# Issuing each half store of the first fourteen sequences as two DMAs of 64 partitions

## Chip, cores, metric

One core of a Trainium2 chip. The metric is the device time of one execution in microseconds, the slowest core's; here there is only one. The "span" of a profile is the part of it that the profiler records, from the first recorded instruction to the last.

## The reference

```python
# indices (32, 512) int32, embedding_table (50000, 512) f32, position_embed (512, 512) f32
def reference(indices, embedding_table, position_embed):
    token_embed = embedding_table[indices]
    return (token_embed + position_embed).astype(np.float32)
```

33.6 MB are gathered in rows of 2 KB, one addition is made on each element, and 33.6 MB are written. The tables and the result lie in HBM ("dram" in the names of the trace); the slots that the gathers fill and the stores read are tiles in SBUF, laid out over 128 partitions (an addition in the trace is 128x512).

## The kernel before

Position p * 4 + k of a sequence lies on partition p. GpSimd issues 128 gathers of 128 rows, VectorE adds the position embedding in place, and the queue of the scalar engine (ScalarE, "ACT") issues the stores. Most stores are "half stores": two of the four k of one sequence, 4 KB on each of 128 partitions, 512 KB.

```python
P = 128; K = 4; SLOTS = 23; LANES = 10; FIRST = 4
# ... tiles, loads of indices and position embedding ...
stores = []
for g, (b, k) in enumerate(order):
    if (b <= 1 and k < half) or b == B - 1:
        stores.append((g + 1, b, k, 1))
    elif k % half == half - 1:
        stores.append((g + 1, b, k + 1 - half, half))
# ...
for g, (b, k) in enumerate(order):                 # GpSimd
    # ... waits for indices; at b == SLOTS for the stores of the slots that are reused
    ins = nc.gpsimd.indirect_dma_start(out=slots[b % SLOTS][:, k, :], in_=table, ...)
    if g >= LANES:
        ins._wait_ge(s_gather[g % LANES], rounds(g - LANES))
# ...
for g, (b, k) in enumerate(order):                 # VectorE
    part = slots[b % SLOTS][:, k, :]
    nc.vector.tensor_tensor(out=part, in0=part, in1=pos_ps[:, k, :], op=add) # waits for gather g
# ...
for adds, b, at, n in stores:                      # ScalarE's queue
    nc.scalar.dma_start(
        out=out_rows[b][:, at : at + n, :],
        in_=slots[b % SLOTS][:, at : at + n, :],
    )._wait_ge(s_add, adds).then_inc(done, 16)
```

## Time and profile before

| | before |
|---|---|
| time, median (3 runs) | 182.06 us |
| span of the profile | 178.8 us |
| GpSimd / VectorE busy | 68% / 51% |
| DMA engines busy, steady stretch | 100% |
| data moved | 68.34 MB, about 418 GB/s from 40 us on |

The prediction below shows the lines behind this table. One more line is needed, the stores as instructions of ScalarE's queue. It reads: line, engine, operation, tile, count, duration of an issue in ns (shortest/median/longest), first and last start in us.

```profile
L160 ACTq DMA_DIRECT2D out_dram<-slot x68: 338/338/372, 8.8 to 170.9; - x68
```

The issues take 338 ns, the longest 372.

### The profile page before, as it was taken

The page shows a single profiled execution, that of the slowest core. Times are in us where ns is not written, and L with a number is a line of the kernel's source. Part 1 is how long each engine was busy: PE and PEld are TensorE (multiplying, and loading weights), DVE is VectorE, ACT ScalarE, POOL GpSimd, SP SyncE. Part 2 cuts the span into 40 slices and gives each one's busy share as a digit, 9 for nine tenths or more (in the row PEclk, how much of TensorE's full clock was granted, in tenths as well). Part 3 has the DMA queues.
Part 4 walks back from the last instruction along what each step waited for, and adds up shares of the span by engine and source line. Part 5 has one row for each costly group of instructions (what it writes and reads, how often), then busy time and mean ns, then how long its engine had stood idle before and what let it go on. Part 6 is the DMA issues. An engine that isn't in the chain of part 4 may idle for free.

```text
span 178.8 us, 399 instructions
## 1 busy us (share of the span) xinstructions
DVE 90.5 (51%) x133; POOL 121.4 (68%) x132
## 2 busy tenths in 40 slices
DVE  0363835555455555555465564556556464555510
POOL 3777777777777777777777777777777777773000
DMA  4999999999999999999999999999999999999950
GB/s 128 305 276 346 331 388 389 411 401 422 415 420 416 419 418 419 420 418 416 420 418 419 418 418 420 414 418 418 420 415 419 420 406 419 417 421 418 414 203 0
DMA packets 21059, 68.34 MB, mean 382 GB/s; under 512 B 3776, under 2 KB 3904, under 8 KB 21056
## 3 DMA queue, kind: packets, MB, share of 16 engines
q0 software_dynamic: 10240, 33.56, 48.3%
q10 hardware_dynamic: 10816, 34.76, 48.3%
q14 instruction: 3, 0.02, 0.0%
HBM read 34.75 MB, written 33.55 MB: 382 GB/s over the span
## 4 chain that ended last, share of the span: by engine, by line
POOL 65%; issue 23%; DMA 6%; DVE 1%; POOLq 1%; ACTq 0%
POOL slot L126 65%; DMA slot<-in_embedding_table_dram,idx_t 5%; DVE slot L151 1%; DMA idx<-in_indices_dram 1%; POOLq L134 1%; ACTq L191 0%; POOLq L97 0%; POOLq L180 0%
## 5 line engine op out<-in xcount | busy, mean ns | idle before, releaser
L126 POOL DMA_INDIRECT slot<-in_embedding_table_dram,idx_t x112 | 105.9, 946 | 34.1 <-issue 34.1
L151 DVE TENSOR_TENSOR slot<-slot,pos_ps 128x512 f32<-128x512 f32 x128 | 87.7, 688 | 75.1 <-issue 61.0
L126 POOL DMA_INDIRECT slot<-in_embedding_table_dram,idx x16 | 15.2, 953 | 7.1 <-issue 4.7
L146 DVE COPY pos_ps<-pos_sb 128x512 f32<-128x512 f32 x4 | 2.8, 688 | 5.2 <-DMA pos_sb<-in_position_embed_dram 5.2
L139 DVE STREAM_TRANSPOSE idx_t<-idx_raw 128x128 int32<-128x128 int32 x1 | 0.4, 401 | 0.0
L180 POOL MEMSET const-float32-0.0<- 128x1 f32 x1 | 0.1, 98 | 0.2 <-issue 0.2
L180 POOL MEMSET const-uint8-127<- 128x1 uint8 x1 | 0.1, 118 | 0.0
L180 POOL MEMSET const-bfloat16-1.0<- 128x1 bf16 x1 | 0.1, 113 | 0.0
L180 POOL MEMSET const-float32-1.0<- 128x1 f32 x1 | 0.1, 104 | 0.0
## 6 DMA issues: line engine op xcount, KB each, us to landing
out_dram<-slot ACTq DMA_DIRECT2D x60, 512.0 KB
out_dram<-slot ACTq DMA_DIRECT2D x8, 256.0 KB
slot<-in_embedding_table_dram,idx_t POOLq DMA_INDIRECT x112
pos_sb<-in_position_embed_dram ACTq DMA_DIRECT2D x2, 512.0 KB
slot<-in_embedding_table_dram,idx POOLq DMA_INDIRECT x16
idx_raw<-in_indices_dram ACTq DMA_DIRECT2D x4, 32.0 KB
idx<-in_indices_dram ACTq DMA_DIRECT2D x1, 4.0 KB, 1.6
idx<-in_indices_dram ACTq DMA_DIRECT2D x1, 12.0 KB
```

The costliest lines, as they stand in the source:

```text
L126: ins = nc.gpsimd.indirect_dma_start(out=slots[b % SLOTS][:, k, :], out_offset=None, in_=table, in_offset=bass.IndirectOffsetOnAxis(ap=whe ...
L134: nc.gpsimd.drain()
L139: nc.vector.transpose(out=idx_t[:], in_=idx_raw[:].rearrange("r (q k w) -> r k q w", k=K, w=2)[:, :, :, 0],)._wait_ge(s_raw, 16 * J).then_ ...
L146: nc.vector.tensor_copy(out=pos_ps[:, k, :], in_=pos_sb[:, k, :])._wait_ge(s_pos[k // half], 16).then_inc(s_ps, 1)
L151: nc.vector.tensor_tensor(out=part, in0=part, in1=pos_ps[:, k, :], op=add)._wait_ge(s_gather[g % LANES], rounds(g)).then_inc(s_add, 1)
L180: nc = _bacc.Bacc("TRN2", target_bir_lowering=False, num_devices=1)
```

## The change

The likely intent is finer pieces of store traffic between the gathers while the pipeline fills. Each half store of sequences 0 to 13 becomes two DMAs, one of partitions 0 to 63 and one of 64 to 127.

```diff
+SPLIT = 14
 ...
-            stores.append((g + 1, b, k, 1))
+            stores.append((g + 1, b, k, 1, slice(0, P)))
         elif k % half == half - 1:
-            stores.append((g + 1, b, k + 1 - half, half))
+            step = P // 2 if b < SPLIT else P
+            stores += [(g + 1, b, k + 1 - half, half, slice(p, p + step))
+                       for p in range(0, P, step)]
 ...
-        for adds, b, at, n in stores:
+        for adds, b, at, n, ps in stores:
 ...
-                out=out_rows[b][:, at : at + n, :],
-                in_=slots[b % SLOTS][:, at : at + n, :],
+                out=out_rows[b][ps, at : at + n, :],
+                in_=slots[b % SLOTS][ps, at : at + n, :],
```

## The prediction

Passages are cut where marked. The sum: 0.2 + 1.0 - 0.3 = +0.9 us, halved to +0.5. Its middle term, the loss of 1 to 3% (1.0 us) for stores of 64 neighbouring partitions, was the author's guess, worked out from no trace; so was the 5% at its edge. "Ports" is the name for this guess.

> **What bounds the kernel now.** I read the page first, then the busy time by stretch, then the timeline at both ends, then the DMA queues of a stretch in the middle. The page says what is full and what isn't:
>
> ```profile
> span 178.8 us, 399 instructions
> DVE 90.5 (51%) x133; POOL 121.4 (68%) x132
> ...
> DMA  4999999999999999999999999999999999999950
> GB/s 128 305 276 346 331 388 389 411 401 422 415 420 416 419 418 419 420 418 416 420 418 419 418 418 420 414 418 418 420 415 419 420 406 419 417 421 418 414 203 0
> DMA packets 21059, 68.34 MB, mean 382 GB/s; under 512 B 3776, under 2 KB 3904, under 8 KB 21056
> ```
>
> The 16 DMA engines are busy from the first slice to the last but two. They reach about 418 GB/s only in the ninth or tenth slice (4.47 us each), and then hold it to the end. No compute engine is full, and the chain of work that ended last goes through GpSimd (65%) and its issue gaps (23%).
>
> GpSimd issues the 128 gathers. The timeline shows its first and last ones:
>
> ```profile
> 2.81 1.08 POOL L126 DMA_INDIRECT slot<-in_embedding_table_dram,idx  x1 [2.36 <-DMA idx<-in_indices_dram]
> 8.08 0.69 DVE L151 TENSOR_TENSOR slot<-slot,pos_ps 128x512 f32<-128x512 f32 x1 [2.18 <-DMA slot<-in_embedding_table_dram,idx]
> ...
> 161.90 0.95 POOL L126 DMA_INDIRECT slot<-in_embedding_table_dram,idx_t  x1 [0.30 <-issue]
> ...
> 170.14 0.69 DVE L151 TENSOR_TENSOR slot<-slot,pos_ps 128x512 f32<-128x512 f32 x1 [0.45 <-issue]
> ```
>
> A gather is 0.95 us and a gap of 0.30, so one each 1.25 us, from the first to the last: (161.90 - 2.81) / 127 = 1.253. That period never stretches, so the wait for the gather ten before, and the wait for the slots to come free, hold up nothing. A gather brings 262,144 bytes; in the same 1.25 us as many bytes must go out. The demand is 2 x 262,144 B / 1.25 us = 419 GB/s, and the DMA moves 418. The two limits are practically equal. From issue to its addition a gather takes 8.08 - 2.81 = 5.3 us at the start, about 7.4 us in the middle (kth gather against kth addition), and 170.14 - 161.90 = 8.2 us at the end: a backlog is built in the first 30 to 40 us and not worked off later. The stretches show where it comes from:
>
> ```profile
> 10.00:15.00 5.00, 2.54 (x4) 3.78 (x5) 1.00 0.95 291
> 20.00:25.00 5.00, 3.48 (x6) 3.78 (x5) 1.00 0.97 323
> 35.00:40.00 5.00, 2.75 (x4) 3.78 (x5) 1.00 1.02 404
> 60.00:100.00 40.00, 21.98 (x32) 30.25 (x33) 1.00 1.03 418
> 163.00:168.00 5.00, 2.73 (x5) 0.00 (x0) 1.00 1.03 420
> ```
>
> (Columns: from and to, us, VectorE busy, GpSimd busy, clock, DMA share, GB/s.) The last row is decisive: GpSimd is done, only backlog is left, and the rate is 420. So 420 is about what the engines can do, against a demand of 419. **Whatever DMA time is lost in the first 80 us can't be won back by the end**; and whatever is gained there can only take backlog away, because GpSimd itself ends at 162.85 whatever the stores do.
>
> [...] the queues get equal shares where stores are issued in one piece:
>
> ```profile
> q0 software_dynamic: 1280, 4.19, 51.6%
> q10 hardware_dynamic: 1147, 4.18, 51.1%
> ```
>
> (DMA queues between 60 and 80 us: packets, MB, share of 16 engines.) [...]
>
> **The change part by part.** Sequences 2 to 13 have two half stores each, and 0 and 1 have one each (their first halves go out in single rows, which aren't split): 26 stores of 512 KB become 52 of 256 KB. They are issued from 8.8 us until the addition of gather 56, which is at 2.8 + 55 x 1.25 + 7.4 = 79 us. Bytes, data packets (4 KB, one per partition), gathers, additions and the order of all else stay.
>
> - *ScalarE's queue.* An issue takes 338 ns; 68 of them are 23.0 us of the span, 94 are 31.8. There are two half stores each 5 us, now 1.35 us of issue in place of 0.68. The queue does nothing else, so this is hidden. A second half starts 0.34 us later than now, and has its first half to run behind. Effect: 0.
> - *Completion packets.* Each DMA ends with 16 small ones. The page's 3776 packets under 512 B are 128 gathers x 16 + 76 plain DMAs x 16 + 512 rows of early indices, exactly. 26 more DMAs add 416. In the trace's packet records a 4-byte packet takes 9 ns: 416 x 9 ns / 16 engines = 0.23 us, most of it where the engines are full, so about **+0.2 us**[...].
> - *Ports.* A data packet of a store takes 16 x 20 us x 0.511 / 1020 = 160 ns (1147 packets less about 127 completions), and a gather's the same. [...] I choose a loss of 1 to 3% of the throughput in the split stretch[...]: 1.4% of 71 us is **1.0 us**, with 0 and 3.5 us (5%) as the edges.
> - *What is gained at the start.* Two smaller DMAs bring no data earlier: a store still waits for its second addition. The page's low slices are a time when too few stores exist, not too slowly issued ones. I put the gain at 0 to **-0.6 us** (a first half that lands a little earlier, packets spread otherwise), -0.3 in the middle.
>
> Sum: 0.2 + 1.0 - 0.3 = +0.9 us. Against it I set that a limit at just the first fourteen sequences looks like a tuned number, chosen because it didn't hurt, and halve it: **+0.5 us, so 182.5 us**.
>
> **The rivals.** *Hidden anyway:* bytes and packets are the same, the engines' shares are the same, the time is 182.1 to 182.4. The equal queue shares speak for it; nothing in the profile speaks against it except that there is no slack to hide anything in. *The ports become the bound:* the split stretch runs at 395 to 405 GB/s, the gather latency grows beyond 8 us and may reach the 12.5 us (ten gathers of 1.25 us) at which GpSimd waits for the gather ten before; 71 us x 4 to 6% is 3 to 4 us: 185 to 186 us. [...] *The split helps:* if the engines' reads are spread better in the first 40 us, the backlog doesn't build. The latency of the last gather could fall from 8.2 us towards the first one's 5.3: 2.9 us at most, 179.2 us. Only the odd number fourteen speaks for it; the packets' unchanged sizes and order against it. *A wait moves:* slot reuse counts the completions of sequences 0 to 8, which end around 55 us, while the gather that waits is number 93, at 118 us. 60 us of slack: nothing.
>
> **Range and chances.** The middle is 182.5. Below it the ceiling of the gain gives 179.2, which I think unlikely, so the lower edge is 180.9; above it a loss of 5% gives 185.8, and the upper edge is 185.3. Two per cent are 3.6 us: faster needs more than the whole backlog, 2.9 us, so 0.03; slower needs a loss of 5% or more all through the stretch, 0.13; the rest, 0.84, is within 2%.
>
> **What would show it.** If the steps hold, the page of the changed kernel has 94 stores, 4192 packets under 512 B and the same bytes; gathers keep 1.25 us; ScalarE's issues stay at about 338 ns. The rate between 40 and 80 us tells the ports: 418 means no collisions, 410 is my middle, 400 and less is the second rival, and then the store packets take over 160 ns there and not after 80 us. The time from the last gather to its addition shows gain or loss directly: 8.2 us now, about 8.7 if I am right, 5 to 7 if the split helps. The prediction would be wrong [...]if a 64-partition store doesn't use all 16 engines evenly, or if the slow start has to do with how large the stores are.

## The result

The changed kernel takes **184.53 us** (median of 4 runs, 184.08 to 184.99), the kernel before 182.12 us (median of 4 runs, 182.01 to 182.2). The ratio is 1.0133, with a 95% interval of 1.0107 to 1.0159. A ratio is the mean time of one kernel's fast runs over that of the other's of the same rounds, so not quite the ratio of the medians quoted. It is a slowdown clear of the noise and inside the 2% that the prediction called "same".

The page of the changed kernel, to be read against the same lines of before:

```profile
span 179.6 us, 425 instructions
DVE 90.6 (50%) x133; POOL 121.7 (68%) x132
...
GB/s 127 297 304 355 324 377 372 382 389 406 401 393 401 399 413 402 419 418 416 413 410 421 419 418 419 421 417 419 422 420 416 421 421 417 419 420 418 418 285 0
DMA packets 21475, 68.34 MB, mean 381 GB/s; under 512 B 4192, under 2 KB 4320, under 8 KB 21472
```

The bytes are the same, the small packets are 416 more, and the compute engines do the same work. Where before reaches 401 to 422 GB/s from the eighth slice on, this one stays at 382 to 413 until the sixteenth (72 us) and then runs at about 418. The stretches of the changed kernel (from and to, us, VectorE busy, GpSimd busy, clock, DMA share, GB/s):

```profile
20.00:40.00 20.00, 11.13 (x17) 15.12 (x17) 1.00 1.00 373
40.00:80.00 40.00, 21.80 (x33) 30.24 (x33) 1.00 1.02 405
80.00:160.00 80.00, 42.92 (x63) 60.50 (x65) 1.00 1.03 418
```

The same three of the kernel before:

```profile
20.00:40.00 20.00, 10.95 (x17) 15.12 (x17) 1.00 1.01 381
40.00:80.00 40.00, 21.99 (x32) 30.25 (x33) 1.00 1.03 418
80.00:160.00 80.00, 43.34 (x63) 60.50 (x65) 1.00 1.03 417
```

Between 40 and 80 us, 13 of 418 GB/s are missing: 40 us x 13/418 = 1.2 us of transfers put off. Between 20 and 40 us it is 20 us x 8/418 = 0.4 us. The DMA share stays at 100% (1.02 against 1.03 from 40 to 80 us): the engines aren't idle, their packets take longer, 163 ns in place of 159 for a store's and 164 in place of 159 for a gather's on average. That is 1.6 of the 2.4 us. The profiled run is the one with the shortest span of the four (179.6 to 181.7 us, mean 180.65), though its time is the longest (184.99 us), so it needn't show the whole loss: its last store ends at 174.4 us, against 173.4 in the profile of before. Stores as instructions, and the last gather and addition, of the changed kernel:

```profile
L163 ACTq DMA_DIRECT2D out_dram<-slot x94: 338/604/2307, 8.6 to 171.8; - x94
```

```profile
162.19 0.94 POOL L129 DMA_INDIRECT slot<-in_embedding_table_dram,idx_t  x1 [0.30 <-issue]
...
171.09 0.69 DVE L154 TENSOR_TENSOR slot<-slot,pos_ps 128x512 f32<-128x512 f32 x1 [0.41 <-issue]
```

GpSimd issues its last gather 0.3 us later than before, and that gather needs 8.9 us to its addition in place of 8.2. The issues of stores, which took 338 to 372 ns, now take 604 in the median and up to 2307 ns. Two things are in this. The shortest issues of a pair of halves take 473 and about 609 ns, which I take as what a pair costs where nothing holds it up. Between 40 and 80 us the median is 1.13 us, and what goes beyond the pair's own cost I take as a queue that is held up.

### The profile page after: what moved, and what is told of

Its sections match the earlier page's. It is cut to its first block, busy times and chain, and to the rows that moved or that the text cites. A ratio compares the mean times of both kernels' runs of the same rounds, so it can differ in the third digit from the quotient of the medians.

```text
span 179.6 us, 425 instructions
## 1 busy us (share of the span) xinstructions
DVE 90.6 (50%) x133; POOL 121.7 (68%) x132
## 2 busy tenths in 40 slices
DMA packets 21475, 68.34 MB, mean 381 GB/s; under 512 B 4192, under 2 KB 4320, under 8 KB 21472
## 4 chain that ended last, share of the span: by engine, by line
POOL 60%; issue 24%; DMA 6%; DVE 5%; POOLq 0%; ACTq 0%
POOL slot L129 60%; DVE slot L154 5%; DMA slot<-in_embedding_table_dram,idx_t 5%; DMA idx<-in_indices_dram 1%; ACTq L194 0%; POOLq L100 0%; POOLq L121 0%; POOLq L183 0%
```

## The experiments

**Theory (ports).** Which partitions a DMA reads sets its rate: engines that read the same 64 neighbouring partitions get in each other's way, engines that read partitions spread over all 128 don't. "Port" names the place where they would meet; no trace records one, so the runs can test the rates but not the place. **Rival (count).** Each extra DMA costs engine or issue time, whichever partitions it takes. **Rival (HBM).** The order in which rows are written to HBM costs.

Three chips, each with the kernel before beside it: 175.93 us on the first, 182.38 and 182.33 us on the other two. So compare within a call. All experiments but the one with stores alone have one edit in common: their last wait, for all stores, is a wait on a constant at the end of ScalarE's program.

```diff
+        nc.scalar.wait_ge(s_rest, 16 * rest)
     tc.no_sync_barrier()
-    nc.scalar.wait_ge(s_rest, nc.scalar.to_reg(16 * rest))
```

All results are right unless "wrong" is said. The last column is the end of the last store packet in the profiled run. It is needed because on the second and third chip the closing instructions after it vary: from it to the end of the span the profiles have 1.5 us on the first chip and 1.4 to 9.6 us on the others, so times and spans there differ by microseconds that are no transfers. Most profiles that aren't from the first chip have 5.2 to 9.6 us; instructions of SyncE take 0.70 us in them (0.70 in before and in the change) that take 0.02 or less on the first chip. But every fourth partition and stores alone, on the same two chips, have 1.6 and 1.4 us. Why is open.

| run | time, us | before | ratio (95%) | GB/s, 40 to 80 us | last store ends, us |
|---|---|---|---|---|---|
| control | 176.21 | 175.93 | 1.0016 (0.9989 to 1.0044) | 415 | 172.7 |
| change again | 179.02 | 175.93 | 1.0169 (1.0136 to 1.0202) | 404 | 175.6 |
| even and odd | 176.30 | 175.93 | 1.0028 (0.9998 to 1.0058) | 415 | 172.4 |
| quarters | 180.82 | 175.93 | 1.0280 (1.0248 to 1.0311) | 388 | 178.5 |
| every fourth | 206.26 | 182.38 | 1.1272 (1.1225 to 1.1320) | 308 | 204.3 |
| HBM in halves | 184.56 | 182.38 | 1.0109 (1.0085 to 1.0133) | 415 | 173.1 |
| SBUF in halves | 185.08 | 182.38 | 1.0142 (1.0116 to 1.0169) | 409 | 175.5 |
| all split | 189.19 | 182.38 | 1.0367 (1.0345 to 1.0388) | 395 | 179.5 |
| control, second | 182.41 | 182.33 | 1.0010 (0.9992 to 1.0027) | 418 | 172.5 |
| HBM in halves, second | 183.98 | 182.33 | 1.0088 (1.0068 to 1.0107) | 417 | 173.3 |
| halves turned | 185.67 | 182.33 | 1.0170 (1.0139 to 1.0200) | 394 | 178.2 |

### Control, and the change again

> A control: the kernel before, only with its last wait (for all stores) written as a wait on a constant at the end of ScalarE's own program, since the form of the original isn't accepted in experiments. Both theories: the same time as the kernel before within 0.3% (181.6 to 182.7 us). Whatever it shows is the base for the other runs.

> The changed kernel with the same rewritten last wait. Both theories: 2.4 us (1.3%) over the control, with 395 to 410 GB/s between 40 and 75 us and about 418 after it.

Both as expected in relation to the kernel before (the control's range in us was meant for a slower chip), with a loss of 179.02 - 176.21 = 2.8 us. On this chip the account closes: against the control the change runs at 371 in place of 390 GB/s from 20 to 40 us (0.9 us of transfers), 404 in place of 415 to 80 us (1.1), and 415 in place of 419 to 160 us (0.8), 2.8 us together, and the last store ends 2.9 us later. The last part is there because held-up halves are still being issued until 90 us: the rate is 398 GB/s from 80 to 92 us, and 418 after.

### Even and odd partitions

```diff
-            step = P // 2 if b < SPLIT else P
-            stores += [(g + 1, b, k + 1 - half, half, slice(p, p + step))
-                       for p in range(0, P, step)]
+            step = 2 if b < SPLIT else 1
+            stores += [(g + 1, b, k + 1 - half, half, slice(p, P, step))
+                       for p in range(step)]
```

> The same number of stores (94) and of completion packets as the change, but the two DMAs take the even and the odd partitions instead of the lower and the upper 64. Port theory [...]: the loss goes, 0 to 0.7 us over the control, 414 GB/s or more between 40 and 75 us. Count theory (each extra DMA costs engine time by its completion packets and its issue): the loss stays, 2.4 us over the control, 400 to 408 GB/s there.

0.1 us over the control: the loss is gone, with as many DMAs and as many completion packets. The queues between 40 and 80 us show it (packets, MB, share of 16 engines). The change again:

```profile
q0 software_dynamic: 2569, 8.43, 54.2%
q10 hardware_dynamic: 2354, 7.70, 48.3%
```

Even and odd:

```profile
q0 software_dynamic: 2540, 8.32, 51.7%
q10 hardware_dynamic: 2522, 8.27, 50.9%
```

Engine time for a MB, the share divided by the MB: stores 6.27 against 6.15, gathers 6.43 against 6.21. So it isn't the stores alone that get slower; the gathers on the same engines pay more. In even and odd both queues move the same amount, in the change the stores fall behind (7.70 MB against 8.27). The count theory is out for this size, on this chip: even and odd was not run on the other two. Since every second partition changes the rows in HBM too, the HBM rival is not out yet.

### Quarters

```diff
-            step = P // 2 if b < SPLIT else P
+            step = P // 4 if b < SPLIT else P
```

> Four DMAs of 32 neighbouring partitions in place of two of 64: 146 stores, 78 more than before instead of 26[...]. Port theory: about the loss of the change, 2 to 4 us over the control. Count theory: three times it, about 7 us over the control.

4.6 us over the control (180.82 - 176.21): more than the port theory's 2 to 4, less than the count theory's 7. Neither hit. The port theory as I had put it doesn't say why quarters, which also read neighbouring partitions of one half, lose 1.8 us more than halves. The completion packets of 52 more DMAs, at the prediction's 9 ns each, come to 52 x 16 x 9 ns / 16 = 0.5 us, an estimate. The next run was to tell whether the number of DMAs is the reason.

### Every fourth partition

The edit of even and odd with 4 in place of 2: 146 DMAs like the quarters, each over all 128 partitions.

> As many DMAs as the quarters (146, 1248 completion packets more than before), but each takes every fourth partition[...]. It separates the two things that grew from halves to quarters. Port theory: 0 to 0.7 us over the kernel before on this chip. If the quarters' extra 1.8 us over the halves came from the number of DMAs (52 more), this one must show three halves of that, about 2.7 us.

Both theories failed outright: 24 us slower. (The profiled run, 207.67 us, counts as slow, being over 1.5% above the fastest of the six, 203.62; the effect is far larger.) The end of this kernel's timeline (start, us, engine):

```profile
170.53 0.69 DVE L154 TENSOR_TENSOR slot<-slot,pos_ps 128x512 f32<-128x512 f32 x1 [0.61 <-DMA slot<-in_embedding_table_dram,idx_t]
170.60 23.19 ACTq L163 DMA_DIRECT2D out_dram<-slot  x23
```

The last addition is done at 171.2 us, and ScalarE's queue still issues stores until 193.8. From about 35 to 148 us it issues one each 1.45 us, 131 KB each, and that is slower than the additions produce them (four each 2.5 us); the DMA share is 0.92 here and its rate 308 GB/s. So here issuing, at 1.45 us a store, is the limit, on a queue that I took to be free. Its store packets are normal between 40 and 80 us, but the gather packets are not: 207 ns on average in place of 159, 16% of them over 200 ns. Which of the two brings on the other isn't shown. Why this form takes 1.45 us from issue to issue when the quarters, as many and as large, went out each 0.77 us on average between 40 and 80 us, no run settles. The run therefore says nothing on ports and nothing on what the quarters lost.

### HBM in halves, SBUF in halves

One side has the change's pattern and the other doesn't. Their outputs are wrong, which doesn't matter for the times.

```diff
+            hbm, sb = [slice(0, 64), slice(64, P)], [slice(0, P, 2), slice(1, P, 2)]   # HBM in halves
+            hbm, sb = [slice(0, P, 2), slice(1, P, 2)], [slice(0, 64), slice(64, P)]   # SBUF in halves
-                out=out_rows[b][ps, at : at + n, :],
+                out=out_rows[b][hs, at : at + n, :],
```

> Wrong on purpose (rows of a half store land in each other's places). The two DMAs write the rows of the lower and the upper half in HBM, as the change does, but read the even and the odd partitions of SBUF. Port theory (the loss is on the SBUF side): no loss, within 0.7 us of the kernel before. HBM theory (the order of the rows written is what costs): the change's loss, about 3 us.

> Wrong on purpose, the other way round: even and odd rows in HBM, lower and upper 64 partitions in SBUF. Port theory: the change's loss, 2.4 to 3.5 us over the kernel before. HBM theory: no loss, within 0.7 us.

SBUF in halves lost 2.7 us, as the port theory has it. But HBM in halves lost 2.2 us where that theory allowed 0.7, so by their times alone the two don't separate. Their traces do. From 40 to 80 us and from 80 to 160 us, first HBM in halves, then SBUF in halves:

```profile
40.00:80.00 40.00, 22.01 (x32) 30.25 (x33) 1.00 1.03 415
80.00:160.00 80.00, 43.40 (x64) 60.50 (x65) 1.00 1.03 419
```

```profile
40.00:80.00 40.00, 21.46 (x32) 30.25 (x33) 1.00 1.03 409
80.00:160.00 80.00, 42.79 (x63) 60.48 (x65) 1.00 1.02 412
```

The first keeps the rate, the second doesn't. In the packet records the last store ends at 173.1 us in the first and at 175.5 in the second.

### Control and HBM in halves, second

> The kernel before with its last wait moved, again, because the two runs with crossed rows had no control on their chip and lasted longer after their last transfer than the kernel before. On a chip where the closing instructions of the SyncE engine take 0.7 us (as in the trace of before) it should be 1.5 to 2.5 us over the kernel before; on one where they take 0.02 us, within 0.5 us of it.

> Wrong on purpose, as before: HBM rows in halves, SBUF partitions even and odd. Port theory: within 0.5 us of control_2, last transfer at 172 to 173.5 us. HBM theory: 2 to 3 us over control_2.

The control missed: the moved wait costs nothing (182.41 against 182.33), although I had expected 1.5 to 2.5 us, so it was not what made HBM in halves longer. HBM in halves again lasts 1.6 us longer in time (0.5 allowed). Its mean span is 179.5 us against the control's 179.2, its rate from 40 to 80 us is 417 against 418, and its last store ends at 173.3 against 172.5 us, because in the profiled run the issue of the very last store came 1.8 us after its addition. So the transfers lose nothing that could be the change's 2 to 3 us, and about 1.3 us of the time lies outside the recorded span, where I can't look. By the time alone the port theory missed with both runs of HBM in halves; that the rows in HBM aren't the cause rests on the rate and on the end of the last store. In the span, SBUF in halves has 182.1 us on average, 2.9 over this control (another chip, with the same time of before within 0.1 us).

### All sequences split

```diff
-SPLIT = 14
+SPLIT = 31
```

> Right results. All sequences but the last are split (60 half stores into 120 in place of 26 into 52). If the loss is a lower rate as long as split stores run, and nothing gives it back: 60/26 of the change's 2.9 us, 6.7 us over the kernel before, with 400 to 408 GB/s until 160 us. If the loss belongs to the start alone (a different build-up of the backlog), it stays at about 3 us.

6.8 us over before, against 6.7 expected from 60/26 of the change's loss. The rate is 395 GB/s from 40 to 80 us and 406 from 80 to 160. So the loss is a lower rate for as long as split stores run, and nothing gives it back. That the times agree to 0.1 us is partly luck: the last store ends 6.1 us later than in the profile of before, and in this profile 9.6 us follow it, in place of 5.4. The path differs, too: the last addition ends at 170.6 us, no later than before's 170.8, so here it is the stores that have fallen behind.

### Stores alone

No gathers, no additions, four stages of 8.4 MB of stores with a wait between. Its output is wrong, which doesn't matter for the time. Every stage writes each row of its sequences in HBM once; the second and the third write their rows in the same order and differ only in the partitions that they read. It ran once.

```diff
+    stages = [[whole], [lower, lower], [lower, upper], [even, odd]]
+        for stage, parts in enumerate(stages):
+            for n in range(16):                     # 16 half stores, each in one or two DMAs
+                ...
+            nc.scalar.wait_ge(s_done, issued)
```

> Wrong on purpose: no gathers and no additions, four stages of 8.4 MB of stores each, one after the other: 16 half stores of 128 partitions; the same as 32 DMAs that all read partitions 0 to 63; 32 that alternate lower and upper half; 32 that alternate even and odd partitions. Port theory: near 400 GB/s in the first and the last stage, about half of it (190 to 220) in the second[...] and something between in the third. Count theory: the last three stages alike, and each only a few per cent below the first.

One stretch of 5 us within each stage (the last number is GB/s):

```profile
15.00:20.00 5.00, 0.00 (x0) 0.00 (x0) 1.00 1.02 406
...
45.00:50.00 5.00, 0.00 (x0) 0.00 (x0) 1.00 0.99 212
...
80.00:85.00 5.00, 0.00 (x0) 0.00 (x0) 1.00 0.82 267
...
115.00:120.00 5.00, 0.00 (x0) 0.00 (x0) 1.00 1.01 401
```

This is the disputed cost by itself. DMAs that read partitions 0 to 63 over and over move 212 GB/s, half of the 406 of whole stores. Lower and upper in turn, as the change issues them, move 267. Even and odd in turn, just as many DMAs of just as many partitions, move 401.

The packet records of these stretches say how. In the first a 4 KB packet takes 160 ns in the median, in the second 305, with the engines still busy (share 0.99): all 16 work, each at half speed. In the fourth it is 162. In the third the median is 159, but 27% of the packets take over 200 ns, and the share is 0.82. So the 267 GB/s come partly from slower packets and partly from engines without work, and why they are without work isn't shown.

### Halves turned

```diff
-                       for p in range(0, P, step)]
+                       for p in range(0, P, step)][:: 1 if (g // half) % 2 else -1]
```

> Right results. The change, but every other half store issues its upper half first[...]. If collisions are eased by engines that have drifted to the other half, drift helps less here: 1.3 to 2 times the change's loss, 4 to 6 us over control_2. If drift plays no part: 2.5 to 3 us over control_2.

By time it is 3.3 us over the control, between the two expectations. By mean span it is 184.1 - 179.2 = 4.9 us over it, and the rate from 40 to 80 us is 394 GB/s where the change had 405 on its chip. Its last store ends 5.8 us after the control's, which would fit the expectation of 4 to 6. So more is lost where two DMAs of the same half follow each other. I call that supported, not settled, since time and span disagree by 1.6 us and there was no run of the change on this chip. That engines drift apart was the author's guess; no trace shows it.

### The packets

The packet records of the traces give the duration of each 4 KB packet. Between 40 and 80 us:

```
                 store packets                      gather packets
                 mean ns   over 200 ns   99th pct   mean ns   over 200 ns
before             159        0.1%         159        159        0.2%
change             163        2.1%         318        164        1.4%
even and odd       159        0.1%         160        161        0.7%
SBUF in halves     161        1.5%         245        163        1.0%
HBM in halves, 2   159        0.0%         159        159        0.2%
quarters           166        3.4%         400        172        3.8%
halves turned      163        2.4%         326        170        3.3%
every fourth       159        0.6%         159        207       15.7%
```

The median is 159 ns everywhere. In the change two store packets of a hundred take much longer. Such store packets are there in every run above that reads 64 or fewer neighbouring partitions of SBUF (1.5 to 3.4% over 200 ns), and all but absent in even and odd (0.1%) and with the halves in HBM only (0.0%). The 318 ns at the 99th percentile mark no doubling (the change on the first chip has 278 there, the quarters 400); the doubling is seen with stores alone, where every DMA reads the same half (305 ns against 160). What such a packet waits for isn't shown; the trace doesn't even say which engine it ran on. And a long tail alone doesn't mark neighbouring partitions: every fourth partition has one in its gathers, for a reason that no run shows.

## Why the prediction was right, and where it was off

The range (180.9 to 185.3 us) and the class held, the range because its upper edge allows for a loss of nearly 5% in the split stretch; the middle of 182.5 was 2 us too low, with +0.5 us in place of the measured +2.4.

- **The bound.** Right. Lost DMA time isn't won back: the loss grows with the number of split stores (6.8 us with all of them), and GpSimd keeps 1.25 us per gather.
- **Ports.** Right in what the runs can show: which partitions a store reads sets its rate. In stores alone it is 212 GB/s for partitions 0 to 63 over and over, 267 for lower and upper in turn, 401 for even and odd, 406 for whole stores. Why isn't shown. The size was off: the prediction put "1.4% of 71 us is 1.0 us". The profile of the change has 405 against 418 GB/s from 40 to 80 us, 3.1%, and the first chip a loss of 2.8 us. The prediction's own band of 1 to 3% had been cut to its lower half; its sign to look for, 410 GB/s as "my middle", would already have been 1.9%.
- **Gain at the start.** Predicted -0.3 us; there is none. From 20 to 40 us the change moves 373 against 381 GB/s, on the other chip 371 against 390.
- **The final halving.** The sum was +0.9 us, and I halved it because fourteen "looks like a tuned number". No trace carried that step, and it took the middle further away from the measured +2.4.
- **Completion packets.** 4192 small packets, exactly as counted. Their cost is too small to see: even and odd is 0.1 us over the control, and its interval against before, 0.0 to +0.6%, leaves room for the predicted 0.2 us and also for none.
- **ScalarE's queue.** The step that failed: "ScalarE's issues stay at about 338 ns". They took 604 ns in the median and up to 2307 ns. An issue of 64 partitions is longer even where nothing holds it up, in the change and in even and odd alike: about 475 ns for the first of a pair and 610 for the second. "Effect: 0" may still hold for that part, since even and odd has as many issues (478 ns in the median) and loses nothing. The rest I take as a consequence of the slower packets; no trace shows what the queue waits for. And in every fourth partition issuing, one store each 1.45 us, was the bound itself.
- **The latency check.** 8.7 us from the last gather to its addition was foretold, 8.9 measured. As the loss was 2.4 us and not the 0.5 behind the 8.7, this hit is luck, or belongs to a profiled run that shows too little of the loss.
- **Rivals.** "Hidden anyway" is out by the interval of the result, "the split helps" by its sign. "The ports become the bound" in its strong form (4 to 6%, gathers waiting for the gather ten before) didn't happen for halves: 267 GB/s of alternating halves alone is more than the 209 (half of 418) that the stores need beside gathers. I take that as the reason why the loss is 1.3% and not half of the rate, an estimate from these two; no run varies it.

## What to carry to other kernels

Where the DMA engines are full, as here at 418 GB/s, ask of each store which partitions it reads, not only how many bytes and DMAs there are: two DMAs of 64 neighbouring partitions cost 1.3% here (1.6% against the control on the first chip), the same two over even and odd partitions nothing measurable on that chip. But one step further, every fourth partition, cost 24 us. In the stretch where the rate dropped from 418 to 405 GB/s the DMA share stayed at 100%: the packets were slower (2.1% of the stores' over 200 ns, before 0.1%), work wasn't missing. In such a stretch look for a tail in their durations. And keep out of a prediction any factor that no view carries, such as a guess at why a constant was chosen.
